# Turning the values and the attention weights by transposing DMAs instead of TensorE, in a two-layer hybrid block

## The chip, the core and the metric

The kernel runs on one core of a Trainium2 chip. A core has five engines that work side by side, each on its own list of instructions in a fixed order: TensorE (PE in the profile: matrix products, its weight loads are the row PEld), VectorE (DVE), ScalarE (ACT), GpSimd (POOL) and SyncE (SP), which here only issues DMAs. Engines wait for each other by semaphores. SBUF is the working memory with 128 partitions; PSUM takes what TensorE writes. The metric is the time of one execution on the device in microseconds; lower is better.

## The reference

The computation is a block of two layers on 272 tokens (16 learned ones and 256 of the input) with 1024 features, all in float32. In each layer the normalized input goes through one wide projection, and its parts feed three branches:

```
rq, rk, rv, rg, hq, hf, hi, hg, dq, dk, dv, mg = split(rms_norm(h) @ w_in)
o_ret = retention(rq, rk, rv, rg)        # 4 heads, values rv
o_hg  = hgrn2(hq, hf, hi, hg)            # 8 heads, a gated recurrence, values hi
o_da  = diff_attention(dq, dk, dv)       # 8 heads: w = softmax(s0) - lam * softmax(s1), then w @ dv
y = sum over the branches of sigmoid(mg_n) * (o_n @ w_branch_n)
h = h + y @ w_out
h = h + conv_ffn(rms_norm(h))            # 5632 wide in, causal convolution of 3, silu gate, 2816 wide out
```

Behind the second layer comes a last normalization. Each branch multiplies some matrix of weights over tokens with its values (`rv`, `hi`, `dv`), so the values are needed with tokens on partitions. The projections come out with features on partitions.

## The kernel before

**The main stream.** All large products run through `products`. A product's weights come as 128x128 tiles, in the order that `ORDER` and `_turns` write out; eight tiles are one chunk of 512 KB. `_Weights.next` (lines 623 to 647) loads a chunk into one of three "wraw" buffers by a DMA on SyncE's queue, ScalarE rounds it to "whi" and VectorE makes the rest, "wlo" (four buffers of each). Three matrix products per tile (lines 912 to 914: high by high, high by low, low by high) keep float32 accuracy. A pair of output tiles takes 16 weight tiles and lands in one of two "main" buffers in PSUM.

**The order.** No instruction is issued as the code meets it. `_Plan.add` notes each operation with its engine, a price and a due time (`key`), and finds what it depends on from the tiles and places it touches (`_span`). `order` (lines 451 to 559) then runs a list schedule: each engine takes what can start first, and of these what is due first, as long as a buffer of each tag is free. Small products on TensorE are due 3 us later than their key, or 8 us earlier when they can stand beside another small one. The prices are in `_Engine` (lines 580 to 604); a copy on GpSimd is taken as 0.04 + 2.45e-3 n us for n elements a partition, a DMA as 0.06 us and its bytes at 360 GB/s, and its result as there 2.0 us after that; a hand-off between engines costs 0.4. The order that comes out is fixed in the program. On the chip an engine whose next instruction isn't ready waits.

**The small work.** It is put in behind projections by the marks in `ORDER` ("+ret" begins the retention heads, "!ret" says where they must end). `behind` chains the pieces of a group: in "da" and "ret" a piece starts only when the last but one is done, so two heads are in flight. `settle` spreads their due times.

**What the change touches.**
- `values` (line 1378): a pair of value tiles (two times 128 features, 272 tokens) is copied out of PSUM into "vsrc", of which there are two buffers. `to_tokens` (line 948) then transposes the first 256 tokens in four blocks on TensorE into a PSUM bank "vt", and ScalarE copies it in two pieces into "vt" or "rvt". The last 16 tokens go another way (`tails`, `tail_tokens`). There are 12 such sets a layer: four each of `rv`, `hi` and `dv`.
- `da_head` (line 1263): the scores (line 1280, tile "ds"), the two softmaxes, whose difference is left in "two_a" on queries by keys (line 1300), `turn` (lines 1304 to 1308), which transposes three 128x128 blocks on TensorE into a bank "wt", two copies on ScalarE into the tile "wts", then the products with the values into "do", the norm of the head (`sub_norm`, with a sum over partitions on GpSimd) and the result in "da". Eight heads a layer, in two groups of four.
- `split_blocks` at the mark "*b2": the two halves of "da" become "b2hi" and "b2lo", which the products of the third branch ("b2") read: for the first eight tiles of a pair the first half, then the second.
- `ret_tail` and `ret_head` (lines 1000 and 1015): the products of the last 16 tokens, copied to `st["ro"]`, and those of the heads, both through the two "acc" banks.
- `SLOTS` (line 39): 14 large buffers shared by most tiles of the mixer and the feed-forward half, among them "vt", "dq", "da", "b2hi", "ghi".

Of the kernel before, what the change touches and what calls it, by code (L numbers as in the profile page):

```python
# [12 lines left out]
F32 = mybir.dt.float32  # L13
F32R = mybir.dt.float32r
U8 = mybir.dt.uint8
AF = mybir.ActivationFunctionType
ALU = mybir.AluOpType
PSUM = bass.MemoryType.PSUM
# [2 lines left out]
P = 128  # L21
DEPTH = 2
META = 16
SEQ = 256
T = META + SEQ
# [10 lines left out]
TAIL = T - 2 * P  # L36
BANK = 512
CHUNK_TILES = 8
SLOTS = 14
LEAD = 6.0  # L40
MARGIN = 12.0
EARLY = 12.0
# [313 lines left out]
class _Plan:  # L356
# [26 lines left out]
    def _span(self, ap):  # L383
        step = ap.ap[0][0]
        lo = ap.offset % step
        hi = lo + 1 + sum((n - 1) * abs(s) for s, n in ap.ap[1:])
        if ap.tensor.name in self.psum:

            lo, hi = lo // BANK * BANK, -(-hi // BANK) * BANK
        return ap.tensor.name, lo, hi  # L390

    def add(self, engine, run, cost, outs, ins, func=None):
# [271 lines left out]
def _trace(ctx, tc, plan, a, depth, probe):  # L664
    nc = tc.nc
# [18 lines left out]
    def new(pool_, shape, dt, tag, bufs, name):  # L684
        serial[0] += 1
        return plan.tile(pool_, shape, dt, tag, bufs, f"{name}_{serial[0]}")
# [16 lines left out]
    def temp2(tag, bufs=2):  # L703
        return temp(2 * T, tag, bufs).rearrange("p (a t) -> p a t", a=2)

    def bank(name):
        return new(bp, [P, 512], F32, "bank", 2, name)
# [34 lines left out]
    ident = const[:, C_IDENT : C_IDENT + P]  # L742
# [201 lines left out]
    def split(hi, lo, x):  # L944
        act.activation(hi, x, AF.Copy)
        tt(lo, x, hi.bitcast(F32), SUB)

    def to_tokens(src, vt, e):

        pt = bank("vt").rearrange("p (f c e) -> p f c e", f=2, c=2)  # L950
        for f in range(2):
            for c in range(2):
                pe.transpose(pt[:, f, c, :], src[:, f, c * P : (c + 1) * P], ident)
        for f in range(2):
            act.activation(vt[:, :, e + f * P : e + (f + 1) * P], pt[:, f], AF.Copy)

    def tail_tokens(tails):

# [21 lines left out]
    for li in range(depth):  # L980
# [19 lines left out]
        def ret_tail():  # L1000

            q, k = (st[n][:, :, 2 * P :].unsqueeze(1).to_broadcast([P, 2, 4, TAIL]) for n in ("rq", "rk"))
            ks = temp(P, "tw")
            twice = lambda t: t.rearrange("p (e h t) -> p e h t", e=2, h=4)
            pool.tensor_copy(twice(ks), k)
            s1 = bank("s1")[:, :P]
            pe.matmul(twice(s1), ks, q, start=True, stop=True)
            w = temp(P, "tw")
            tt(w, s1, const[:, C_DECT : C_DECT + P], MUL)
            o = acc_bank("ro")[:, :P]  # L1010
            pe.matmul(o, st["rvs"], w, start=True, stop=True)
            st["ro"] = temp(P, "tw")
            act.activation(st["ro"], o, AF.Copy)

        def ret_head(hd):
            q, k, vt, gate = st["rq"], st["rk"], st["rvt"], st["rg"]
            if hd == 0:
                st["dec"] = slot4("dec")
                sync.dma_start(st["dec"].rearrange("p h t -> p (h t)"), a["dec"])
            dec = st["dec"][:, hd, :]  # L1020

            s1 = bank("s1")
            a1 = temp(T + P + TAIL, "wts")
            parts = ((0, t0, t0, dec[:, t0:]), (P, P, T, dec[:, : P + TAIL]))
            for k0, q0, at, _ in parts:
                pe.matmul(s1[:, at : at + T - q0], k[:, hd, k0 : k0 + P], q[:, hd, q0:], start=True, stop=True)
                plan.hold(a1)
            for _, q0, at, by in parts:
                tt(a1[:, at : at + T - q0], s1[:, at : at + T - q0], by, MUL)
            os = [acc_bank("ro") for _ in range(2)]  # L1030
            sq = temp2("sum", 1)
            for e in range(2):
                o = os[e]
                ec = slice((hd * 2 + e) % 4 * P, (hd * 2 + e) % 4 * P + P)
                v = vt[(hd * 2 + e) // 4]
                pe.matmul(o[:, t0:T], v[:, 0, ec], a1[:, t0:T], start=True, stop=False)
                pe.matmul(o[:, P:T], v[:, 1, ec], a1[:, T : T + P + TAIL], start=False, stop=True)
            for e in range(2):
                i = (e * 4 + hd) * TAIL
                tt(os[e][:, 2 * P : T], os[e][:, 2 * P : T], st["ro"][:, i : i + TAIL], ADD)  # L1040
            for e in range(2):
                act.activation(sq[:, e, t0:], os[e][:, t0:T], AF.Square)
            tt(sq[:, 0, t0:], sq[:, 0, t0:], sq[:, 1, t0:], ADD)
            r = temp(T, "hr")
            inverse(r[:, t0:], sq[:, 0, t0:], 2 * P)
            for e in range(2):
                g = gate[:, hd * 2 + e, t0:]
                y = temp(T, "ho")[:, t0:]
                tt(y, os[e][:, t0:T], r[:, t0:], MUL)
                tt(g, y, g, MUL)  # L1050
# [212 lines left out]
        def da_head(b, hd):  # L1263
            q, k, vt, out = st[f"dq{b}"], st[f"dk{b}"], st[f"dvt{b}"], st[f"da{b}"]
            scale = DA_DH ** -0.5

            a1 = temp(T + P + TAIL, "wts")
            pool.tensor_copy(a1[:, :META], st[f"dw{b}"][:, hd * META : (hd + 1) * META])
            tiles = ((META + P, T, 0), (META, META + P, T))
            sb = [temp(2 * T, tag) for tag in ("two_a", "two_b")]  # L1270
            ss = [bank("ds") for _ in range(2)]
            red = temp(12, "dm")
            nm, sm, cf = (red[:, 4 * i : 4 * i + 4].rearrange("p (t m) -> p t m", m=2) for i in range(3))


            def scores():
                for q0, nk, at in tiles:
                    for m in range(2):
                        half = slice(64 * m, 64 * m + 64)
                        nc.tensor.matmul(ss[m][:, at : at + nk], q[half, hd, q0 : q0 + P], k[half, hd, :nk], start=True, stop=True)  # L1280

            plan.add("pe", scores, 0.95, [x[:, : T + P + META] for x in ss], [q[:, hd, :], k[:, hd, :]])
            plan.hold(*sb, a1)
            for i, (q0, nk, at) in enumerate(tiles):
                mask = const[:, C_MASK + T - nk : C_MASK + T]
                for m in range(2):
                    cols = slice(at, at + nk)
                    dve.tensor_tensor_reduce(out=sb[m][:, cols], in0=ss[m][:, cols], in1=mask, scale=1.0,
                                             scalar=-3e38, op0=ADD, op1=ALU.max, accum_out=nm[:, i, m : m + 1])
            ts(nm, nm, -scale, None, MUL)  # L1290
            for i, (q0, nk, at) in enumerate(tiles):
                for m in range(2):
                    p = sb[m][:, at : at + nk]
                    act.activation(p, p, AF.Exp, bias=nm[:, i, m : m + 1], scale=scale, accum_out=sm[:, i, m : m + 1])
            dve.reciprocal(cf, sm)
            tt(cf[:, :, 1], cf[:, :, 1], nlam[:, li : li + 1].to_broadcast([P, 2]), MUL)
            for i, (q0, nk, at) in enumerate(tiles):
                p0, p1 = (x[:, at : at + nk] for x in sb)
                ts(p1, p1, cf[:, i, 1:2], None, MUL)
                stt(p0, p0, cf[:, i, 0:1], p1, MUL, ADD)  # L1300
            w = sb[0]
            wt = bank("wt")

            def turn(wt=wt, w=w):
                for i, c in enumerate((0, P, T)):
                    nc.tensor.transpose(wt[:, i * P : (i + 1) * P], w[:, c : c + P], ident)

            plan.add("pe", turn, 0.33, [wt[:, : 3 * P]], [w[:, : T + P]])
            act.activation(a1[:, META + P : T + P], wt[:, : 2 * P], AF.Copy)
            act.activation(a1[:, META : META + P], wt[:, 2 * P : 3 * P], AF.Copy)  # L1310

            for g, c in ((0, 2 * P), (1, T + P)):
                pool.tensor_copy(st[f"dt{b}"][:, g, hd, :], w[:, c : c + TAIL])
            o = acc_bank("do")
            ec = slice(hd * P, hd * P + P)
            pe.matmul(o[:, t0:T], vt[:, 0, ec], a1[:, t0:T], start=True, stop=False)
            pe.matmul(o[:, P + META : T], vt[:, 1, ec], a1[:, T : T + P], start=False, stop=True)
            for g, c in ((0, 2 * P), (1, P)):
                act.activation(st[f"do{b}"][:, g, hd, :], o[:, c : c + TAIL], AF.Copy)
            sub_norm(out[:, hd, t0 : 2 * P], o[:, t0 : 2 * P])  # L1320
# [56 lines left out]

        def values(ps, vt, e):

            src = temp2("vsrc")  # L1380
            evacuate(src, ps)
            plan.key += 2.0
            to_tokens(src, vt, e)
            return src
# [234 lines left out]
```

## Time and profile before

| | |
|---|---|
| time, median of 3 runs | 1308.54 us (1308.46 to 1308.67) |
| the profiled execution | 1308.31 us, of which the span from first to last instruction is 1306.5 us |
| granted TensorE clock | 0.999 |
| value sets, attention heads | 24 and 16 in all |
| share of the span in which the DMA engines moved data | 49% |

A row of a group or a tile tells the line, the engine, the operation, what it writes and reads, the count and the durations in nanoseconds (a mean, or least, median and most). A row of the waits tells who waited for whom, for how many microseconds in total, how many times, and the longest. A row of the timeline gives the start and the length in microseconds; with "x4" several equal ones are merged. All that goes through the helper stands under line 604, so the tiles' names tell what it is. TensorE's matmuls overlap, so their spacing counts and not their length.

### The profile page before, as it was taken

The numbers are of one execution on the slowest core, as the hardware profiler recorded it, in microseconds if no ns is written. First come the engines' busy times: TensorE is split into PE (matmuls) and PEld (weight loads), VectorE is DVE, ScalarE is ACT, GpSimd is POOL, SyncE is SP. The second block draws the span as 40 slices with busy tenths as digits, with TensorE's granted clock in tenths as the row PEclk, the third lists the DMA queues.
The fourth block names the chain that finished last, engine by engine and source line by source line (L and its number), as shares of the span: only waits on it lengthen the run. The fifth ranks groups of instructions, "written<-read, shape, count | busy, mean of one in ns | idle before, by whom it ended". The sixth has DMA issues, their size and how long they took to land.

```text
span 1306.5 us, 28679 instructions
## 1 busy us (share of the span) xinstructions
PE 1294.6 (99%) x11774; PEld 1265.6 (97%) x11774; DVE 958.4 (73%) x1589; ACT 800.5 (61%) x1328; POOL 168.6 (13%) x204
## 2 busy tenths in 40 slices
PE   9999999999999999999999999999999999999998
PEld 9999999999999999999999999999999999999986
DVE  7675777698586789886575767876985867898843
ACT  6846454756576567666456564657565765776643
POOL 5001111222122020000030011012130220200000
PEclk9999999999999999999999999999999999999999
DMA  7644543443534545555555445444445445465553
GB/s 271 200 148 161 169 156 130 162 146 123 184 136 158 181 156 178 189 167 185 175 177 188 164 148 177 148 147 160 146 144 180 139 162 202 145 208 196 200 189 111
DMA packets 60755, 219.06 MB, mean 168 GB/s; under 512 B 6864, under 2 KB 6992, under 8 KB 60624
## 3 DMA queue, kind: packets, MB, share of 16 engines
q1 hardware_dynamic: 60336, 216.71, 49.0%
q8 instruction: 92, 1.51, 0.5%
q10 hardware_dynamic: 288, 0.52, 0.1%
q14 instruction: 39, 0.32, 0.1%
HBM read 216.16 MB, written 1.05 MB: 166 GB/s over the span
## 4 chain that ended last, share of the span: by engine, by line
PE 92%; DVE 5%; issue 1%; ACT 1%; DMA 0%; SPq 0%; DVEq 0%; ACTq 0%
PE main L912 27%; PE main L914 27%; PE main L913 26%; PE fo L1420 2%; PE fo L1419 2%; PE fo L1418 2%; DVE two_b L604 1%; PE lev L1096 1%; DVE two_a L604 1%; DVE wlo L604 1%; PE ds L1280 1%; PE vt L604 1%; PE ro L604 1%; PE ho L604 1%; PE do L604 1%
## 5 line engine op out<-in xcount | busy, mean ns | idle before, releaser
L912 PE MATMUL main<-xh,whi 128*128 128x272 f32 (+1 forms) x2368 | 682.0, 288 | 0.0
L913 PE MATMUL main<-xl,whi 128*128 128x272 f32 (+1 forms) x2368 | 672.5, 284 | 1.5 <-DVE xl L604 1.5
L914 PE MATMUL main<-xh,wlo 128*128 128x272 f32 (+1 forms) x2368 | 673.1, 284 | 0.9 <-DVE wlo L604 0.5
L604 DVE TENSOR_TENSOR wlo<-wraw,whi 128x1024 fp32r<-128x1024 f32 (+1 forms) x411 | 501.9, 1227 | 202.9 <-ACT whi L604 202.2
L604 ACT ACTIVATE whi<-wraw 128x1024 fp32r<-128x1024 f32 (+1 forms) x411 | 427.6, 1043 | 244.5 <-PE main L913 167.1
L914 PEld LDWEIGHTS main<-xh,wlo 128*128 128x128 f32 x2368 | 445.8, 188 | 2.7 <-DVE wlo L604 2.7
L913 PEld LDWEIGHTS main<-xl,whi 128*128 128x128 f32 x2368 | 446.1, 188 | 2.2 <-DVE xl L604 1.9
L912 PEld LDWEIGHTS main<-xh,whi 128*128 128x128 f32 x2368 | 446.1, 188 | 1.0
L604 DVE SCALAR_TENSOR_TENSOR two_b<-main,small,two_b 128x256 f32<-128x256 f32 (+2 forms) x144 | 65.3, 486 | 24.8 <-ACT two_b L604 23.1
L604 POOL PARTITION_ALL_REDUCE hr<-hsq x36 | 67.5, 1886 | 117.0 <-ACT hsq L604 116.2
L604 POOL TENSOR_TENSOR y<-h,rstd 128x272 f32<-128x272 f32 x32 | 34.6, 1112 | 318.1 <-ACT rstd L604 318.1
L604 ACT ACTIVATE two_b<-main,small 128x272 f32<-128x272 f32 (+1 forms) x72 | 37.3, 566 | 24.3 <-PE main L914 23.3
L912 PE MATMUL main<-ghi,whi 128*128 128x272 f32 x176 | 51.0, 290 | 0.0
L913 PE MATMUL main<-glo,whi 128*128 128x272 f32 x176 | 50.6, 287 | 0.0
L914 PE MATMUL main<-ghi,wlo 128*128 128x272 f32 x176 | 50.3, 286 | 0.0
L604 POOL COPY tails<-vsrc 128x32 f32<-128x32 f32 x32 | 10.1, 330 | 225.0 <-ACT vsrc L604 224.9
L912 PE MATMUL main<-b0hi,whi 128*128 128x272 f32 (+1 forms) x128 | 37.9, 296 | 0.0
L912 PE MATMUL main<-b1hi,whi 128*128 128x272 f32 (+1 forms) x128 | 37.8, 296 | 0.0
L912 PE MATMUL main<-yhi,whi 128*128 128x272 f32 (+1 forms) x128 | 36.4, 284 | 0.0
L914 PE MATMUL main<-yhi,wlo 128*128 128x272 f32 (+1 forms) x128 | 36.4, 284 | 0.0
L913 PE MATMUL main<-b1lo,whi 128*128 128x272 f32 (+1 forms) x128 | 36.3, 284 | 0.0
L914 PE MATMUL main<-b1hi,wlo 128*128 128x272 f32 (+1 forms) x128 | 36.3, 284 | 0.0
(236 smaller groups left out, 1915.9 us busy)
## 6 DMA issues: line engine op xcount, KB each, us to landing
wraw<-in_w SPq DMA_DIRECT2D x402, 512.0 KB, 3.3
h<-in_h SPq DMA_DIRECT2D x4, 272.0 KB, 5.3
dec<-in_dec SPq DMA_DIRECT2D x2, 544.0 KB, 4.2
wraw<-in_w SPq DMA_DIRECT2D x4, 256.0 KB, 4.5
const<-in_const SPq DMA_DIRECT2D x1, 937.0 KB, 6.1
gain<-in_gl SPq DMA_DIRECT2D x1, 512.0 KB, 5.5
out<-y ACTq DMA_DIRECT2D x2, 256.0 KB, 3.0
out<-y SPq DMA_DIRECT2D x2, 256.0 KB, 2.9
```

The costliest lines, as they stand in the source:

```text
L604: self.plan.add(self.name, lambda: f(*args, **kw), cost, outs, ins, args[2] if method == "activation" else None)
L912: nc.tensor.matmul(o, wh, hi, start=first, stop=False)
L913: nc.tensor.matmul(o, wh, lo, start=False, stop=False)
L914: nc.tensor.matmul(o, wl, hi, start=False, stop=last)
L1096: nc.tensor.matmul(o, keys, x, start=True, stop=True)
L1280: nc.tensor.matmul(ss[m][:, at : at + nk], q[half, hd, q0 : q0 + P], k[half, hd, :nk], start=True, stop=True)
L1418: nc.tensor.matmul(o, gh, wh, start=False, stop=False)
L1419: nc.tensor.matmul(o, gl, wh, start=False, stop=False)
L1420: nc.tensor.matmul(o, gh, wl, start=False, stop=end)
```

## The change

Both turns leave TensorE. A float32 tile is seen as pairs of 16-bit halves. Two copies on GpSimd (four in an attention head, whose source has two pieces) part it into a plane of the low halves and a plane of the high halves ("apart"). Two transposing DMAs on SyncE's queue, one for each plane, write the blocks transposed ("turned"). Two copies on GpSimd put the halves together again in the place where ScalarE had copied from PSUM. The PSUM banks "vt" and "wt" of these steps and the copies by ScalarE are gone.

With it: "apart" and "turned" are buffers of the tag "vsrc", which has now four instead of two; each large buffer is as big as two of them, and `SLOTS` goes from 14 to 13. `_span` halves the places of 16-bit tiles. A retention head's first product now waits until the copy of the tail's product is done.

```diff
-SLOTS = 14
+SLOTS = 13
@@ _span
+        if ap.dtype == U16:
+            lo, hi = lo / 2, hi / 2
@@
+    def planes(name, n):
+        return new(tp, [P, 4 * T], U16, "vsrc", 4, name)[:, : 2 * n].rearrange("p (i x) -> p i x", i=2)
+
+    def halves(t):
+        return t.bitcast(U16).rearrange("p (x two) -> p x two", two=2)
+
     def to_tokens(src, vt, e):
-        pt = bank("vt").rearrange("p (f c e) -> p f c e", f=2, c=2)
-        for f in range(2):
-            for c in range(2):
-                pe.transpose(pt[:, f, c, :], src[:, f, c * P : (c + 1) * P], ident)
-        for f in range(2):
-            act.activation(vt[:, :, e + f * P : e + (f + 1) * P], pt[:, f], AF.Copy)
+        apart, turned = planes("apart", 4 * P), planes("turned", 4 * P)
+        for i in range(2):
+            pool.tensor_copy(apart[:, i].rearrange("p (c f x) -> p c f x", c=2, f=2),
+                             halves(src.rearrange("p f t -> p (f t)"))[:, :, i].rearrange("p (f t) -> p f t", f=2)[:, :, : 2 * P].rearrange("p f (c x) -> p c f x", c=2))
+        for i in range(2):
+            sync.dma_start(turned[:, i].rearrange("p (b x) -> p b x", x=P), apart[:, i], transpose=True)
+        for i in range(2):
+            pool.tensor_copy(vt.bitcast(U16).rearrange("p c (x two) -> p c x two", two=2)[:, :, e : e + 2 * P, i], turned[:, i].rearrange("p (c x) -> p c x", c=2))
@@ ret_tail
             act.activation(st["ro"], o, AF.Copy)
+            st["rot"] = plan.ops[-1]
@@ ret_head
                 pe.matmul(o[:, t0:T], v[:, 0, ec], a1[:, t0:T], start=True, stop=False)
+                plan.queue(plan.ops[-1], st["rot"])
@@ da_head
             w = sb[0]
-            wt = bank("wt")
-            def turn(wt=wt, w=w):
-                for i, c in enumerate((0, P, T)):
-                    nc.tensor.transpose(wt[:, i * P : (i + 1) * P], w[:, c : c + P], ident)
-            plan.add("pe", turn, 0.33, [wt[:, : 3 * P]], [w[:, : T + P]])
-            act.activation(a1[:, META + P : T + P], wt[:, : 2 * P], AF.Copy)
-            act.activation(a1[:, META : META + P], wt[:, 2 * P : 3 * P], AF.Copy)
+            apart, turned = planes("apart", 3 * P), planes("turned", 3 * P)
+            for i in range(2):
+                for c, n, at in ((0, 2 * P, P), (T, P, 0)):
+                    pool.tensor_copy(apart[:, i, at : at + n], halves(w[:, c : c + n])[:, :, i])
+            for i in range(2):
+                sync.dma_start(turned[:, i].rearrange("p (b x) -> p b x", x=P), apart[:, i], transpose=True)
+            for i in range(2):
+                pool.tensor_copy(halves(a1[:, META : T + P])[:, :, i], turned[:, i])
@@ values
-            src = temp2("vsrc")
+            src = temp2("vsrc", 4)
```

1 line of the change is left out of this document (added).

## The prediction

> **What bounds the kernel now.** I read the page first (busy time, the chain that ended last), then the waits, and then the timeline of the places the change touches.
>
> ```profile
> span 1306.5 us, 28679 instructions
> PE 1294.6 (99%) x11774; PEld 1265.6 (97%) x11774; DVE 958.4 (73%) x1589; ACT 800.5 (61%) x1328; POOL 168.6 (13%) x204
> PE 92%; DVE 5%; issue 1%; ACT 1%; DMA 0%; SPq 0%; DVEq 0%; ACTq 0%
> ```
>
> TensorE is busy 99% of the span and carries 92% of the chain. A TensorE instruction that goes away is worth its time, and a microsecond in which TensorE waits is lost. GpSimd has room, 13% busy. What feeds TensorE is the weight stream:
>
> ```profile
> SPq L604 <- DVE wlo L604: 780.0, 279, 7.7
> ACT whi L604 <- PE main L913: 167.1, 141, 3.0
> ACT whi L604 <- DMA wraw<-in_w: 17.2, 14, 3.4
> PEld main L914 <- DVE wlo L604: 2.7, 9, 0.5
> ```
>
> ```profile
> q1 hardware_dynamic: 60336, 216.71, 49.0%
> ```
>
> The columns are total microseconds, times, longest. SyncE's queue mostly stands before a load whose raw buffer is still being split (780 us). ScalarE waits for TensorE to free a split buffer ten times as long as for a load, so the weights are ahead of their use, and TensorE hardly waits for them (2.7 us). The transfers of that queue fill the DMA engines to 49%.
>
> **What goes.** The sets of transposes, with the ordinary matmuls around them:
>
> ```profile
> L604 PE MATMUL vt<-const,vsrc x96: 270/272/329, 77.8 to 994.4; 128*128 128x128 f32 x96
> L1306 PE MATMUL wt<-const,two_a x48: 270/272/330, 294.0 to 1047.3; 128*128 128x128 f32 x48
> 160.14 0.29 PE L913 MATMUL main<-xl,whi 128*128 128x272 f32 x1
> 160.26 0.29 PE L914 MATMUL main<-xh,wlo 128*128 128x272 f32 x1
> 160.39 0.60 PE L604 MATMUL vt<-const,vsrc 128*128 128x128 f32 x4
> 160.74 0.37 PE L912 MATMUL main<-xh,whi 128*128 128x272 f32 x1
> 293.90 0.29 PE L914 MATMUL main<-b0hi,wlo 128*128 128x272 f32 x1
> 294.03 0.49 PE L1306 MATMUL wt<-const,two_a 128*128 128x128 f32 x3
> 294.27 0.37 PE L912 MATMUL main<-b0hi,whi 128*128 128x272 f32 x1
> PEld wt L1306 <- DVE two_a L604: 3.1, 6, 0.7
> ```
>
> Matmuls overlap, so the price is read from start to start. From 160.26 to 160.74 is 0.48 us where two ordinary matmuls are 0.12 apart: a values set costs 0.36 us. There are 96 / 4 = 24 sets: 8.6 us. An attention set costs 294.27 - 293.90 - 0.12 = 0.25 us, 48 / 3 = 16 sets: 4.0 us. The waits of these sets for the weights' last product (3.1 us, 6 times) go with them. Sum of the gain: 15.7 us. ScalarE loses the copies out of PSUM, but it is not the bound, and I count nothing for it.
>
> **What comes.** Each turn becomes copies on GpSimd (parting), two transposing DMAs on SyncE's queue, and copies on GpSimd (joining). The nearest rows:
>
> ```profile
> 178.82 0.21 POOL L604 COPY tails<-vsrc 128x32 f32<-128x32 f32 x1 [6.45 <-ACT vsrc L604]
> 824.25 0.29 POOL L604 COPY tw<-rk 128x128 f32<-128x128 f32 x1
> 170.59 1.05 POOL L604 COPY tails<-vsrc 128x32 f32<-128x32 f32 x1 [6.19 <-ACT vsrc L604]
> 170.28 1.28 DVE L604 TENSOR_TENSOR hq<-hq,he 128x1088 f32<-128x1088 f32 x1
> L604 POOL TENSOR_TENSOR y<-h,rstd 128x272 f32<-128x272 f32 x32 | 34.6, 1112 | 318.1 <-ACT rstd L604 318.1
> small<-in_small SPq DMA_DIRECT2D x1, 16.0 KB, 1.7
> wraw<-in_w SPq DMA_DIRECT2D x402, 512.0 KB, 3.3
> DMA to landing us min/median/max: 3.0/3.3/6.4
> L604 SPq DMA_DIRECT2D wraw<-in_w x406: 327/328/716, 1.6 to 1283.7; - x136
> L604 ACT ACTIVATE vsrc<-main x6: 624/627/628, 155.4 to 193.1; 128x544 f32<-128x544 f32 x6
> ```
>
> A GpSimd copy: 0.21 us at 32 elements and 0.29 at 128, so 0.18 + 0.83 ns an element. That gives 0.39 us at 256, 0.50 at 384 and 0.61 at 512. The copy at 170.59 took 1.05 us instead of 0.21: it started inside VectorE's product of two SBUF tiles and ended with it. VectorE is 73% busy; I take half of such a delay, 0.42 us, for each copy. The ends are no delay, and the two-input row (1112 ns at 272, so 4.1 ns an element, 2.1 us at 512).
>
> A transposing DMA is nowhere in the trace. A plane is 128 KB (values) or 96 KB. The fastest row is the 16 KB load, 1.7 us; the slowest on this queue is a weight load, 6.4 us. I take the ordinary weight load, 3.3 us: it moves more bytes, but the planes move in far smaller pieces. I take the two planes of a turn one after the other, 6.6 us, since both pass one queue. The ends are 1.7 + 0.33 (one issue) = 2.0 us and 2 x 6.4 = 12.8 us.
>
> [...]
>
> *Values.* Per layer 12 sets, 6 of them in one row, 155.4 to 193.1, 7.5 us apart. GpSimd gets 4 x (0.61 + 0.42) = 4.1 us a set, SyncE's queue 6.6 us: both fit in 7.5. The users come late enough:
>
> ```profile
> 81.50 0.21 POOL L604 COPY tails<-vsrc 128x32 f32<-128x32 f32 x1 [7.05 <-ACT vsrc L604]
> L604 PE MATMUL ho<-at,vt x64: 258/280/286, 106.1 to 920.7; 128*128 128x144 f32 x32, 128*128 128x128 f32 x16, 128*128 128x114 f32 x16
> L604 PE MATMUL ro<-wts,rvt x64: 284/332/395, 209.3 to 894.8; 128*128 128x144 f32 x32, 128*128 128x272 f32 x16, 128*128 128x258 f32 x16
> ```
>
> The second set of the gated recurrence is in SBUF by 81.5, and the first product with such values ("ho") starts at 106.1, 25 us later. The first retention product starts at 209.3 and reads the first two sets of its four, in SBUF at 170.6 and 178.8: 30 us. A turn of 4.1 + 6.6 us fits, and I count nothing. What hides it is this lead, and three of the four "vsrc" buffers a set; without it the next set stays in PSUM and TensorE stops. A weight load queued behind a transposing DMA that waits for GpSimd is late by the same time; the lead of the weights shown above hides single delays.
>
> *Attention heads.* Here the turn lies on a chain that is waited for:
>
> ```profile
> 292.93 0.37 DVE L604 SCALAR_TENSOR_TENSOR two_a<-two_a,dm,two_b 128x144 f32<-128x144 f32 x1
> 296.23 0.84 PE L604 MATMUL do<-wts,vt 128*128 128x272 f32 x4
> 366.31 0.85 PE L1280 MATMUL ds<-dk,dq 64*128 64x272 f32 x6
> 411.38 1.29 DVE L604 TENSOR_TENSOR b2lo<-da,b2hi 128x1088 fp32r<-128x1088 f32 x1
> 420.27 0.29 PE L912 MATMUL main<-b2hi,whi 128*128 128x272 f32 x1
> 1061.30 1.23 DVE L604 TENSOR_TENSOR b2lo<-da,b2hi 128x1032 fp32r<-128x1032 f32 x1
> 1067.38 0.28 PE L912 MATMUL main<-b2hi,whi 128*128 128x258 f32 x1
> ```
>
> Before, from the weights' end (293.30) to the head's output product (296.23) is 2.9 us. After: the first plane's two copies 0.39 + 0.29 + 2 x 0.42 = 1.5 (the second plane's lie beside the first transfer); SyncE standing before a load, half of 780 / 279 us = 1.4; transfers 6.6; joining the second plane 0.50 + 0.42 = 0.9; hand-offs 0.3. Together 10.7 us, so a head grows by 7.8 us (ends: 0.7 + 2.0 + 0.5 + 0.3 - 2.9 = +0.6, and +15 with 12.8 for the transfers and full delays).
>
> At most two heads are in flight, so a group of four takes two rounds and grows by 15.6 us. The second group's result is ready at 412.7. The third branch's products begin at 420.3 and reach that half after 8 tiles x 3 x 0.12 = 3 us, at 423.2: 10.5 us of cover, less 1.5 that TensorE no longer spends on turns meanwhile, 9.0. In the second layer it is ready at 1062.5 and needed at 1070.2: 7.7 - 1.5 = 6.2 us. TensorE so stops for 15.6 - 9.0 = 6.6 and 15.6 - 6.2 = 9.4 us, 16 together.
>
> The first group has no such end, but TensorE's order is fixed beforehand by the planner's prices (lines 585 to 603, and 2.0 us after a DMA). With them this chain is 2 x 1.02 (parting) + 0.6 + 2.0 (the second DMA) + 0.98 (joining) + 4 x 0.4 (hand-offs) = 7.2 us, 3.5 short of mine, so TensorE meets the output product too early. Before, its prices were short by about 1 us a head (1.9 of 2.9), and 16 turns cost the 3.1 us above: 0.2 of the difference. Once per pair at full price would be 4 x 3.5 = 14 us, a fifth per head 8 x 3.5 x 0.2 = 5.6; I take the middle, 10 us. On GpSimd a joining copy that waits for its DMA holds up what stands behind it, the tail copies and the other head's all-reduce; that is in the upper end, not in the sum.
>
> *The rest.* The edit that lets a retention head wait for the copy of the tail's output holds back two products by at most the copy, 0.5 us once a layer; the planner has ordinary matmuls to put there: 0, up to 1. Thirteen slots: the feed-forward half holds six "ghi" and six "glo", 12, and I count no more elsewhere: 0; were the cover gone, a result would stay in PSUM.
>
> **Sum**: 1308.3 (the profiled execution, 0.2 below the median 1308.5) - 15.7 + 16 + 10 = 1318.6, say 1319 us.
>
> **The rivals.** *The turn is as quick as a small load* (other side). With 2.0 us for the pair, the head's chain is 1.5 + 1.4 + 2.0 + 0.9 + 0.3 = 6.1, +3.2. Two rounds, 6.4 us, stay within the cover in layer one and miss it by 0.2 in layer two, and the planner's 7.2 us is enough: 1308.3 - 15.7 = 1292.6, say 1294. For it: the queue's DMA engines are half idle, and only the transfer has to be quick. Against it: even a plain 512 KB load takes 3.3 us. The point where it decides: the loss is 4g - 15.2 (the two covers) + 2.9(g - 4.3) for a head grown by g (2.9 being 10 / 3.5, and 4.3 the planner's 7.2 - 2.9), and it equals 15.7 at g = 6.3, a pair of 5.1 us. [...]
>
> *Both cancel*: g near 6.3, 1306 to 1311.
>
> *SyncE's queue becomes the bound.* At 6.4 us a plane a values set holds the queue 12.8 us where 7.5 are there; six sets miss 32 us. The weight loads stand behind them; three raw buffers at 1306 / 406 = 3.2 us a load cover 10, so 22 us a layer are lost. The heads grow by 14.0, which by the formula above loses 41 + 28 against the gain of 15.7: 1308 + 44 + 53 = some 1405 us. For it: one queue in order. Against: a plain load's issue holds SyncE 0.33 us only.
>
> *GpSimd is late*: at 2.1 us a copy a set needs 8.4 us for parting where 7.5 are there, and a head grows by some 3 more (4.1 ns an element, full delays): by the formula about 1340.
>
> **Chances.** Forecast (1311 to 1345) 0.40, quick turn 0.27, cancelling 0.08, queue 0.20, GpSimd 0.05. Range 1293 to 1380: it takes in the quick turn and leaves out most of the queue's case; the forecast's own is 1311 to 1345. A change under 0.2% (2.6 us) can't be told from none. Faster 0.27, same 0.08, slower 0.65.
>
> **What would show it.** Right: no "vt" and no attention "wt" transposes on TensorE, 15 us less busy; TensorE waits at "do" and before "b2hi"; a head's weights-to-output time near 11 us; GpSimd's copies 0.4 to 1.0 us. Wrong: transposing DMAs landing under 2.5 us (faster), or holding SyncE for microseconds, with "wraw" waited for by ScalarE (much slower); a wait at "main" for a PSUM buffer during the values would contradict my zero there.

## The result and the profile after

The changed kernel takes 1326.68 us (median of 5 runs, 1323.02 to 1328.93), the kernel before 1308.54 us (1308.46 to 1309.06): a ratio of 1.013, with a 95% interval of 1.0118 to 1.0141. It is 18.1 us slower. The execution that was profiled took 1323.02 us, the fastest of the five, 14.7 us more than the profiled execution before (1308.31). What is read below from the two traces accounts for the 14.7 us; the rest of the 18.1 is in executions that have no trace.

First the page of the changed kernel, the lines that answer to those shown of before.

```profile
span 1321.2 us, 28630 instructions
...
PE 1284.1 (97%) x11630; PEld 1253.8 (95%) x11630; DVE 985.0 (75%) x1589; ACT 778.7 (59%) x1250; POOL 334.8 (25%) x396
...
PE 81%; DVE 7%; POOL 4%; ACT 3%; DMA 3%; issue 1%; SPq 0%; DVEq 0%; ACTq 0%; POOLq 0%
```

TensorE lost 144 matmuls and is 10.5 us less busy, and yet its share of the chain that ended last fell from 92% to 81%. GpSimd (4%) and the DMA (3%) now stand on that chain. VectorE, which got no instruction more, is 26.6 us busier.

Next the waits of TensorE in the changed kernel (total microseconds, times, longest). The prediction showed, on its weight loads, only 2.7 us for a weight half and 3.1 us for the turns.

```profile
PE main L915 <- ACT b2hi L607: 10.7, 2, 6.0
PE do L607 <- DVE tw L607: 4.7, 2, 3.2
PE lev L1109 <- DVE hf L607: 3.1, 2, 1.6
PE vm L607 <- POOL tails L607: 2.5, 4, 1.1
PE main L916 <- DVE b2lo L607: 1.7, 2, 1.1
PE do L607 <- POOL wts L607: 1.7, 3, 0.7
PE lev L1109 <- DVE hq L607: 1.0, 1, 1.0
```

Two groups stand out. The third branch's products wait for the second group of heads, once in each layer: 10.7 + 1.7 = 12.4 us. And products in the section of the values wait for VectorE and for GpSimd's tail copies (those of the recurrence, "lev", and the transposes of the last 16 tokens' values, "vm"): 3.1 + 1.0 + 2.5 = 6.6 us, with shorter ones of the kind ("ho" 0.8 among them) 8.2 us. The prediction's sum had the first and not the second. Before, the waits of this engine over 0.5 us in all were these three, beside one at the start:

```profile
PE wt L1306 <- DVE two_a L604: 1.6, 4, 0.5
PE main L913 <- DVE xl L604: 1.5, 2, 1.1
...
PE do L604 <- DVE tw L604: 0.8, 1, 0.8
```

The transposing DMAs (tile "turned"; durations of the issue, then the time to landing), and after them one of GpSimd's groups of copies, kept apart by shape:

```profile
L607 SPq DMA_TRANSPOSE turned<-apart x80: 1183/1196/2983, 74.8 to 1068.0; - x80
...
DMA to landing us min/median/max: 2.3/3.7/6.5
```

```profile
L607 POOL COPY apart<-vsrc 128x512 uint16<-128x512 uint16 x48 | 45.0, 957 | 144.9 <-ACT vsrc L607 144.7
```

A transposing DMA holds SyncE for 1.2 us, where a weight load held it for 0.33, and lands 3.7 us after its issue. None lands in less than 2.3 us, and in the median a plane takes about as long as a weight load with at least four times its bytes (3.6 us in this trace). The planes move in small packets: SyncE's queue moves 39424 packets and 9.44 MB more than before (99760 and 226.15 MB), 239 bytes a packet, where before a packet had 3.6 KB in the mean. In the run below with the heads alone attention planes land in 3.5 us in the median and 2.3 at least; the 20 values planes that the changed kernel issues before 290 us land in 3.9 and 2.4.

The first head, in the timeline of the changed kernel (start, length):

```profile
292.98 0.40 POOL L607 COPY apart<-two_a 128x256 uint16<-128x256 uint16 x1 [5.76 <-DVE two_a L607]
...
293.60 1.94 POOL L607 COPY apart<-two_a 128x128 uint16<-128x128 uint16 x3 [0.22 <-DVE two_a L607]
...
293.93 1.20 SPq L607 DMA_TRANSPOSE turned<-apart  x1
...
295.80 1.19 SPq L607 DMA_TRANSPOSE turned<-apart  x1
...
296.29 0.63 POOL L607 COPY wts<-turned 128x384 uint16<-128x384 uint16 x1 [0.47 <-DMA turned<-apart]
...
298.35 2.44 DVE L607 TENSOR_TENSOR wlo<-wraw,whi 128x1024 fp32r<-128x1024 f32 x2
298.49 2.57 POOL L607 COPY apart<-two_a 128x128 uint16<-128x128 uint16 x2 [0.22 <-DVE two_a L607]
...
301.01 0.63 POOL L607 COPY wts<-turned 128x384 uint16<-128x384 uint16 x1
...
302.46 0.84 PE L607 MATMUL do<-wts,vt 128*128 128x272 f32 x4
```

The first plane is joined 2.4 us after its DMA was issued. The second plane's joining copy starts at 301.01, 5.2 us after its own (295.80), and it did not wait for the transfer to the end: GpSimd came to it straight from the parting copies of the next head, which took 2.57 us for two (298.49) beside VectorE's products "wlo" of two SBUF tiles (298.35 to 300.79). The output product follows at 302.46. Over all 16 heads the way from the weights' end to that product is 10.57 us in the mean; before it was 2.75. This head is not the typical one. Over the 15 heads whose planes can be told apart from those of the values, the two transfers take 6.3 us in the mean, from the first issue to the second landing, since the second plane's DMA is issued 2.5 us after the first's; from the last landing to the copy that joins it 0.9 us go by.

What the wait before the third branch does, in layer 1. First the timeline of TensorE (its last row is of layer 2), then the windows (length, busy time and count of TensorE and of its weight loads, of VectorE, ScalarE, GpSimd; granted clock; DMA share; GB/s).

```profile
428.54 0.59 PE L915 MATMUL main<-b2hi,whi 128*128 128x272 f32 x1 [4.66 <-ACT b2hi L607]
430.19 0.60 PE L916 MATMUL main<-b2lo,whi 128*128 128x272 f32 x1 [1.06 <-DVE b2lo L607]
430.59 0.43 PE L917 MATMUL main<-b2hi,wlo 128*128 128x272 f32 x1
430.81 0.43 PE L915 MATMUL main<-b2hi,whi 128*128 128x272 f32 x1
...
434.67 0.30 PE L917 MATMUL main<-b2hi,wlo 128*128 128x272 f32 x1
...
1079.27 0.49 PE L607 MATMUL do<-tw,vs 128*128 128x128 f32 x2 [3.18 <-DVE tw L607]
```

```profile
423.60:427.80 4.20, 0.29 (x3) 0.07 (x1) 1.57 (x3) 4.16 (x6) 0.41 (x2) 1.00 0.00 0
427.85:434.65 6.80, 5.05 (x20) 4.75 (x21) 2.29 (x2) 0.64 (x1) 0.00 (x0) 0.50 0.46 157
434.70:440.00 5.30, 5.30 (x44) 5.30 (x44) 4.56 (x7) 2.78 (x3) 0.00 (x0) 1.00 0.16 39
1079.80:1090.00 10.20, 3.56 (x15) 3.27 (x16) 3.46 (x5) 2.88 (x6) 2.32 (x4) 0.50 0.31 103
```

TensorE stands for 4.66 us, and the granted clock falls to 0.50, 4.0 us into the stop. When work comes again, matmuls follow each other every 0.227 us (430.59 to 430.81, to 434.67) instead of every 0.12, until 434.67: the clock is back at 1.00, 6.1 us after work began. Layer 2 has the same, for over 10 us; there the wait of a tail's product (3.18 us, at 1079.27) leads straight into that for the second group (6.0 us). From 430.59 to 434.67 are 18 matmuls at 0.107 us too much, 1.9 us; the same reading of 1087.40 to 1089.98 in layer 2 gives 1.2 us.

So the profiled difference adds up: -12.6 (40 sets of transposes, at the prediction's prices) - 2.4 (waits of before that are gone or shorter, "wt" and "xl") + 12.4 (before the third branch) + 5.6 ("do", 4.7 + 1.7 against 0.8) + 8.2 (the values' section) + 3.1 (half clock) = 14.3 us, against 14.7 measured.

### The profile page after: what moved, and what is told of

Same layout as the page of the kernel before. It is cut to its first block, busy times and chain, and to the rows that moved or that the text cites. A ratio compares the mean times of both kernels' runs of the same rounds, so it can differ in the third digit from the quotient of the medians.

```text
span 1321.2 us, 28630 instructions
## 1 busy us (share of the span) xinstructions
PE 1284.1 (97%) x11630; PEld 1253.8 (95%) x11630; DVE 985.0 (75%) x1589; ACT 778.7 (59%) x1250; POOL 334.8 (25%) x396
## 3 DMA queue, kind: packets, MB, share of 16 engines
q1 hardware_dynamic: 99760, 226.15, 56.7%
## 4 chain that ended last, share of the span: by engine, by line
PE 81%; DVE 7%; POOL 4%; ACT 3%; DMA 3%; issue 1%; SPq 0%; DVEq 0%; ACTq 0%; POOLq 0%
PE main L915 24%; PE main L916 24%; PE main L917 24%; DVE wlo L607 2%; POOL apart L607 2%; DMA turned<-apart 2%; PE fo L1430 2%; PE fo L1431 2%; PE fo L1432 2%; PE ds L1293 1%; PE ho L607 1%; PE lev L1109 1%; PE ro L607 1%; ACT whi L607 1%; DVE two_b L607 1%
## 5 line engine op out<-in xcount | busy, mean ns | idle before, releaser
L607 DVE TENSOR_TENSOR wlo<-wraw,whi 128x1024 fp32r<-128x1024 f32 (+1 forms) x411 | 514.9, 1258 | 183.0 <-ACT whi L607 180.4
L607 POOL PARTITION_ALL_REDUCE hr<-hsq x36 | 70.2, 1966 | 81.4 <-ACT hsq L607 81.4
L607 POOL COPY apart<-vsrc 128x512 uint16<-128x512 uint16 x48 | 45.0, 957 | 144.9 <-ACT vsrc L607 144.7
L607 POOL COPY apart<-two_a 128x256 uint16<-128x256 uint16 x64 | 40.6, 660 | 58.6 <-DVE two_a L607 58.6
L915 PE MATMUL main<-b2hi,whi 128*128 128x272 f32 (+1 forms) x128 | 38.4, 300 | 10.7 <-ACT b2hi L607 10.7
L607 POOL COPY vt<-turned 128x512 uint16<-128x512 uint16 x32 | 33.4, 1056 | 26.5 <-DMA turned<-apart 26.2
L916 PE MATMUL main<-b2lo,whi 128*128 128x272 f32 (+1 forms) x128 | 38.3, 299 | 1.7 <-DVE b2lo L607 1.7
L917 PE MATMUL main<-b2hi,wlo 128*128 128x272 f32 (+1 forms) x128 | 37.7, 295 | 0.0
```

The source lines that it names most:

```text
L607: self.plan.add(self.name, lambda: f(*args, **kw), cost, outs, ins, args[2] if method == "activation" else None)
L915: nc.tensor.matmul(o, wh, hi, start=first, stop=False)
L916: nc.tensor.matmul(o, wh, lo, start=False, stop=False)
L917: nc.tensor.matmul(o, wl, hi, start=False, stop=last)
```

## The experiments

Each is compared with the kernel before on the same chip; its median lay between 1308.46 and 1308.62 in all of them. My theory was that the heads' longer chain makes the loss and the values' part is a gain; the rivals stand in each expectation.

**Values alone, and heads alone.** The old transposes were put back in `da_head`, and in the other run in `to_tokens`:

```diff
# values_only: da_head as before
-            apart, turned = planes("apart", 3 * P), planes("turned", 3 * P)
...
+            wt = bank("wt")
+            plan.add("pe", turn, 0.33, [wt[:, : 3 * P]], [w[:, : T + P]])
...
# attention_only: to_tokens as before
-        apart, turned = planes("apart", 4 * P), planes("turned", 4 * P)
...
+        pt = bank("vt").rearrange("p (f c e) -> p f c e", f=2, c=2)
...
```

> Values turned by DMA as in the changed kernel, attention weights turned on TensorE as before. Theory (the loss is the attention heads' longer chain, which ends in TensorE's wait before the third branch's products; the values' turn lies beside other work): 24 sets x 0.36 us less on TensorE and no wait before the third branch, 1298 to 1303 us. Rival (the values' copies and transposing DMAs cost as well, by late weight loads or late consumers): 1308 us or more.

> Attention weights turned by DMA as in the changed kernel, values on TensorE as before. Theory (heads' chain): both waits before the third branch's products stay, and the 8.6 us of the values' sets are back on TensorE: 1328 to 1337 us. Rival (values and attention share the loss): under 1322 us.

Measured: values alone 1305.82 us (1303.55 to 1306.51; ratio 0.9977, 0.9967 to 0.9987), heads alone 1321.72 us (1320.96 to 1322.30; 1.0099, 1.0082 to 1.0116). The heads carry the loss, and their trace has the waits before "b2" (12.4 us) and the half clock of the changed kernel. But both numbers are off: the values bring 2.8 us of the 8.6 that their transposes cost, the heads alone lose 13.1 where I expected some 20 or more, and the two together (10.3) explain 18.1 badly. The trace of the values alone shows where their gain is eaten. First its timeline, then one VectorE product from it and the same one from the kernel before (busy time, mean ns):

```profile
169.74 0.76 PE L1109 MATMUL lev<-hq,hf 128*32 128x32 f32 x64 [0.90 <-DVE hq L607]
...
180.21 0.73 PE L1109 MATMUL lev<-hq,hf 128*32 128x16 f32 x64 [1.49 <-DVE hf L607]
...
740.37 1.88 POOL L607 COPY vt<-turned 128x512 uint16<-128x512 uint16 x1 [0.16 <-DMA turned<-apart]
...
741.53 1.24 DVE L607 TENSOR_TENSOR hq<-hq,tot 128x544 f32<-128x544 f32 x1
```

```profile
L607 DVE TENSOR_TENSOR hq<-hq,tot 128x544 f32<-128x544 f32 x12 | 10.4, 865 | 0.0
```

```profile
L604 DVE TENSOR_TENSOR hq<-hq,tot 128x544 f32<-128x544 f32 x12 | 8.6, 717 | 0.0
```

The same product of two SBUF tiles lasts 865 ns in the mean instead of 717, and the first matmuls of a level of the recurrence wait for it and for its like ("hf"). The mean hides two cases. The eight of the twelve that no GpSimd copy meets last 712 to 722 ns, as before; the four that start while one of GpSimd's copies runs last 1034 to 1242 ns, and each ends 0.5 to 0.6 us after that copy (741.53 above: the copy ends at 742.25, the product at 742.77). So in these four VectorE stands until the copy is through. The prediction had counted that VectorE delays GpSimd, and not that GpSimd delays VectorE.

**The values' copies on ScalarE.** The DMAs stay, and the four copies of a values set leave GpSimd; the heads are as before.

```diff
# to_tokens, against values_only
-            pool.tensor_copy(apart[:, i].rearrange(...), halves(...)...)
+            act.activation(apart[:, i].rearrange(...), halves(...)..., AF.Copy)
...
-            pool.tensor_copy(vt.bitcast(U16).rearrange(...)[...], turned[:, i].rearrange(...))
+            act.activation(vt.bitcast(U16).rearrange(...)[...], turned[:, i].rearrange(...), AF.Copy)
```

> Values turned by DMA, attention weights on TensorE, and the four copies of a values set moved from GpSimd to ScalarE. Theory (GpSimd's copies hold up VectorE's products of two SBUF tiles, which the gated recurrence's small products on TensorE wait for): VectorE's hq by tot product falls back from 0.87 to 0.72 us, TensorE's waits before lev go, 1299 to 1304 us. Rival (those waits come from the transposing DMAs or from an out-of-date order): the waits stay, 1304 to 1308 us; more if ScalarE's roundings of the weights get late.

Measured: 1301.03 us (1297.95 to 1302.81; ratio 0.9938, 0.9925 to 0.9950). The product by line and shape, from this kernel:

```profile
L607 DVE TENSOR_TENSOR hq<-hq,tot 128x544 f32<-128x544 f32 x12 | 8.6, 718 | 0.0
```

It is back at 718 ns, the same transposing DMAs notwithstanding, and the gain is 7.6 us of 8.6. So for the values the copies on GpSimd are the cause, not the transfers. This version, with the heads on TensorE as before, is 25.7 us faster than the changed kernel.

**No transposing DMA in the heads.** GpSimd's copies stay, and the joining copies read the parted planes. The attention weights are left unturned here.

```diff
# against attention_only
-            for i in range(2):
-                sync.dma_start(turned[:, i]..., apart[:, i], transpose=True)
...
-                pool.tensor_copy(halves(a1[:, META : T + P])[:, :, i], turned[:, i])
+                pool.tensor_copy(halves(a1[:, META : T + P])[:, :, i], apart[:, i])
```

> Attention weights parted and joined by GpSimd as in the run with attention alone, but the joining copies read the parted planes and no transposing DMA is issued: the weights are left unturned, so the attention's output is another. Theory (the DMA pair with its queue is some 6 of the 7.8 us by which a head grew): from weights to output product 4 to 6 us, no wait before the third branch's products, 1304 to 1310 us. Rival (the copies and VectorE's hold-ups make the head late): still above 1314 us.

Measured: 1303.91 us (1301.78 to 1304.47; ratio 0.9961, 0.9947 to 0.9974), just under what I expected. The way from the weights to the output product is 5.30 us (9.93 with the DMAs), and TensorE waits for nothing before the third branch. Of the waits at the heads these are left:

```profile
PE do L607 <- POOL wts L607: 1.8, 1, 1.8
PE do L607 <- DVE tw L607: 1.5, 1, 1.5
```

The two transfers alone, 4.6 us a head, turn a gain of 4.7 us into a loss of 13.1. GpSimd's copies in the heads cost little by themselves.

**Idle time filled.** With the heads alone turned, constant products keep TensorE at work where it stood: 12 behind the tails' transpose and 20 before the awaited tile of the third branch.

```diff
# against attention_only
+    def filler(n, behind):
+        t = bank("fill")
+        def run():
+            for _ in range(n):
+                nc.tensor.matmul(t[:, :P], ones_d, ones_d, start=True, stop=True)
+        op = plan.add("pe", run, 0.214 * n, [t[:, :P]], [ones_d])
...
+                filler(12, [plan.ops[-1]])
...
+                fill = filler(20, [plan.main[-1], st["dax"]])
```

> The run with attention alone, with products of constants in TensorE's list where it waits for the last heads (12 behind the transpose of the tails, 20 before the waited-for tile). Theory (the half clock behind the wait comes from TensorE standing idle for some 4 us): the granted clock stays full and the third branch begins no later, 4 to 6 us less, 1315 to 1318 us. Rival (it comes from the transposing DMAs or the load): the half clock stays, 1321 us or more.

Measured: 1317.17 us (1316.43 to 1318.48; ratio 1.0066, 1.0052 to 1.0080), 4.6 us less than without the filling. Its timeline at the same place, and its windows:

```profile
423.67 4.63 PE L936 MATMUL fill<-ones_d 128*128 128x128 f32 x40
428.06 0.38 PE L915 MATMUL main<-b2hi,whi 128*128 128x272 f32 x1
...
430.77 0.29 PE L915 MATMUL main<-b2hi,whi 128*128 128x272 f32 x1
430.93 0.40 PE L916 MATMUL main<-b2lo,whi 128*128 128x272 f32 x1
```

```profile
423.60:435.00 11.40, 11.40 (x96) 11.31 (x96) 4.87 (x6) 7.91 (x8) 0.41 (x2) 1.00 0.35 119
1070.00:1090.00 20.00, 20.00 (x176) 20.00 (x175) 11.11 (x15) 13.06 (x18) 3.23 (x4) 1.00 0.31 109
```

The transposing DMAs are the same, and the clock stays at 1.00: the half clock comes from TensorE standing idle. The products at 428.06 are not the awaited ones yet. In both runs 48 products of the third branch need only the first half; in layer 1 the planner put 21 of them behind the filling. The 49th, the first that was waited for, starts at 430.77 in layer 1 (427.64 unfilled) and at 1081.96 in layer 2 (1083.83). So the filling moves more than the clock, and the 4.6 us are not the half clock's price alone. The spacing gives that price: unfilled, the 105 products from 429.29 on take 15.60 us and the 143 from 1085.10 on 19.17, where at the spacing of the kernel before they would take 12.9 and 16.7. The two stops cost some 5 us beside their own 12.4.

**The planner's prices.** Is the order bad because the planner doesn't know the long chain?

```diff
+            if outs[0].dtype == U16 or ins and ins[0].dtype == U16:
+                cost = 1.2 if method == "dma_start" else 0.18 + 0.83e-3 * n + 0.4
...
-            done = t + cost + (2.0 if e == "sp" else 0.0)
+            done = t + cost + (2.0 if e == "sp" else 0.0) + (0.5 if op.func == "turn" else 0.0)
```

> The changed kernel, with the planner told what the trace showed: a transposing DMA holds the queue 1.2 us and lands 2.5 us after, a copy of 16-bit halves takes 0.58 + 0.83e-3 n us. Theory: the small waits of TensorE at out-of-date places (some 10 us in all) shrink, the wait before the third branch stays: 1315 to 1323 us. Rival (the wrong prices cause the wait before the third branch too): under 1312 us.

Measured: 1331.58 us (1330.71 to 1332.87; ratio 1.0176, 1.0161 to 1.0192). A miss: it got slower. Its waits:

```profile
PE main L917 <- ACT b2hi L609: 12.7, 2, 6.5
PE do L609 <- POOL wts L609: 8.6, 3, 3.3
PE main L917 <- ACT vsrc L609: 3.1, 1, 3.1
```

With the true prices the chain from weights to output product got longer (13.49 us in the mean instead of 10.57) and the output products wait more, not less; a product of the main stream now also waits for a values tile to leave PSUM (3.1 us). That TensorE meets the output products too early because of outdated prices is not borne out. The edit changes the order of all engines, though, so it does not test TensorE's places by themselves.

**Earlier places for the second group.** `settle` spreads the jobs of a section; a job's due times start behind its own beginning by as many steps as jobs stand ahead of it, those counted that began long before.

```diff
                 begin = max(begin, mine[0][1])
+                i -= sum(x[1] < begin for x in mine)
```

> The changed kernel, but the due times of the second group of four heads begin at their own start and not six steps later, some 10 to 15 us earlier. Theory (heads' chain too long for the room before the third branch): the wait before the third branch goes in the first layer and shrinks in the second, and the half clock behind it with it: 1302 to 1314 us, with the head's time from weights to output product still near 10.5 us. Rival (waits elsewhere carry the loss): above 1320 us.

Measured: 1313.98 us (1312.89 to 1315.20; ratio 1.0041, 1.0026 to 1.0056), 12.7 us less than the changed kernel by the medians (7.8 by the two profiles), at the upper edge of what I expected. Layer 1 has no wait before the third branch any more; layer 2 still has one of 5.7 us. The chain itself is as long as in the changed kernel (10.62 us), so what it costs is a matter of when it starts.

**Buffers alone.**

```diff
# against the kernel before
-SLOTS = 14
+SLOTS = 13
...
+            st["rot"] = plan.ops[-1]
...
+                plan.queue(plan.ops[-1], st["rot"])
...
-            src = temp2("vsrc")
+            src = temp2("vsrc", 4)
```

> The kernel before with 13 large buffers, four vsrc buffers and the retention heads' wait for the tail's copy, and nothing turned by DMA. Theory (buffers and that wait cost nothing): 1308 to 1309.5 us. Rival (a missing large buffer moves work): 1310 us or more.

Measured: 1308.12 us (1307.67 to 1308.98; ratio 0.9998, 0.9988 to 1.0007). They cost nothing.

**The whole change with both cures.** The values' copies on ScalarE, alone and with the earlier places; the edits are those of the runs above, against the changed kernel.

```diff
# all_scalar, and all_scalar_early
-            pool.tensor_copy(apart[:, i].rearrange(...), ...)
+            act.activation(apart[:, i].rearrange(...), ..., AF.Copy)
...
# all_scalar_early only
+                i -= sum(x[1] < begin for x in mine)
```

> The whole change, with the values' four copies a set on ScalarE instead of GpSimd; the heads keep theirs on GpSimd. Theory (the heads' late result sets the time of both layers' attention sections, and the values' copies on GpSimd lengthen VectorE's products beside them and the heads' chains with them): the values then add nothing of their own, and the time is that of the attention part alone or a little under, 1316 to 1322; the products hq<-hq,tot at 544 elements last about 0.72 us. Rival (the 5 us that the values add on top of the attention part come from the shared SyncE queue, where the values' transposing DMAs stand): it stays at 1324 to 1328.

> As the run beside it, and the second group of heads in each layer gets its places in TensorE's order from its own beginning. Theory: both losses shrink, so the time lies under that of the earlier places alone (1314.0) by what the values' copies on GpSimd cost, 2 to 6 us: 1307 to 1312, no gain left over the kernel before, because layer 2 keeps its wait before the third branch (about 3 us or more, and half clock behind it). Rival (with GpSimd free the heads get quick enough): no wait of over 1 us before b2hi in either layer, 1298 to 1304.

Measured: 1312.83 us (1312.27 to 1318.00; ratio 1.0044, 1.0028 to 1.0060) and 1300.19 us (1296.86 to 1302.23; ratio 0.9934, 0.9914 to 0.9953). Both are under what the theory said. The first falls 8.9 us below the heads alone, nearly the 8.6 of the values' transposes: with the copies off GpSimd the two parts add up (-7.6 and +13.1 make +5.5, and +4.4 was measured), and my idea that a wait at the end of the section swallows whatever the values win falls. In the changed kernel the same 96 copies cost 13.9 us by the medians, 7.7 by the two profiles. In the second the rival held: no product waits for "b2hi" in either layer. From its page:

```profile
PE 1280.9 (99%) x11630; PEld 1252.5 (96%) x11630; DVE 963.9 (74%) x1589; ACT 831.1 (64%) x1344; POOL 228.9 (18%) x300
```

TensorE is busy 99% of the span again, 13.7 us less than before the change, and VectorE is back from 985 to 964 us. This version does all that the change set out to do and is 8.3 us faster than the kernel before.

**Controls for the order.** The earlier places in the kernel before, and with the values' part alone.

```diff
# before_early: before.  values_scalar_early: values_scalar
                 begin = max(begin, mine[0][1])
+                i -= sum(x[1] < begin for x in mine)
```

> The kernel before with one thing changed: the second group of heads gets its places in TensorE's order from its own beginning. It tells whether the order alone is worth anything, or only mends what the longer heads lost. Theory (before, the second group's result was 7 to 10 us early, so no wait is there to be mended): the same, 1306 to 1311. Rival (the crowded places cost the kernel before too): under 1305.

> The values turned by transposing DMAs with copies on ScalarE, the heads' weights turned on TensorE as before, and the earlier places for the second group of heads. Beside the run of the whole change with both edits (1300.2) it tells what the attention part is worth once nothing waits for its result. Theory (16 sets off TensorE at 0.25 us are 4.0 us): it is slower than that run by 2 to 5 us, 1301 to 1305. Rival (the attention part brings nothing even then, the order is what helps): it is at 1297 to 1300.

Measured: 1309.30 us (1309.02 to 1309.59; ratio 1.0005, 0.9996 to 1.0015) and 1301.88 us (1300.73 to 1303.13; ratio 0.9949, 0.9934 to 0.9964). The order is worth nothing by itself; it mends only what the longer heads lost. The heads' part on top of the values' (1301.88 to 1300.19) brings 1.7 us of its 4.0, within the spread of both. So the fastest two versions, the values alone with copies on ScalarE (1301.03) and the whole with both cures (1300.19), can't be told apart.

## Why the prediction was right, and where it was not

The forecast was slower, 1319 us; it is slower, 1326.7. Its main mechanism was there and some of its terms were well sized, but two steps failed. That the sum is only 8 us low is in part luck: the 10 us for the order are some 2.4 on the trace, and the values' 8.2 us and the half clock's 3.1 stood at nothing.

- *The gain, 15.7 us.* Right. The transposes are gone. That TensorE is only 10.5 us less busy, and not 15, fits the longer matmuls at half clock (0.43 us in layer 1 instead of 0.29); where the stops are mended it is 13.7 us less.
- *A head grows from 2.9 to 10.7 us.* Right: 10.57. The pair of transfers was put at 6.6 us and takes 6.3 in the mean, though not for the reason given. The second plane does not stand behind the first's transfer: its DMA is issued 2.5 us after the first's, once its copies are done and SyncE is free. SyncE's queue costs 1.2 us a head (1.4 foreseen), at the second plane and not at the first; this is the mean of the 16 heads with the values on TensorE. What the sum left out is GpSimd's queue: 0.9 us in the mean between the last landing and its joining copy, and up to 3.3, as the joining stands behind the next head's parting. I had put that into the upper end alone. That the transfers are what tips it is shown: without them a head needs 5.30 us, and the time is below the kernel before.
- *16 us before the third branch.* Right as a place, in both layers: 12.4 us, and with the tail's wait that leads into it in layer 2 (3.2 us) 15.6. That it comes so near is luck as well. In layer 1 the second half is ready 17.5 us later than before (430.1 instead of 412.7) and not 15.6, while TensorE has more to do until then: the planner put the first half of the next pair ahead, 48 products instead of the 24 counted, 3 us more of cover in each layer.
- *10 us for outdated places in TensorE's order.* This step failed. The waits at the output products grew by 5.6 us, most of it (4.7) at the tails' products "do<-tw"; without the 3.2 us that belong to the stop in layer 2 it is 2.4. And true prices made the kernel slower, not faster. What in the order does cost is another thing: the second group of heads starts late. Moved forward it gives back 12.7 us.
- *Values: "a turn fits, and I count nothing".* This step failed, and it is the largest miss. The lead of the values did hide the turns. The copies on GpSimd cost VectorE, whose products of two SBUF tiles stand until a running copy ends (717 ns alone, 1034 to 1242 behind a copy) with the recurrence waiting for them, and they hold up the tail copies in GpSimd's queue (TensorE's "vm" waits 2.5 us for those, and did not before). Taking them off GpSimd gives 13.9 us by the medians, 7.7 by the two profiles.
- *A stop costs its own length.* Nothing in the sum stood for the half clock behind it: 3.1 us in the profiled execution by the spacing of its matmuls, some 5 us in the run with the heads alone.
- *Buffers, slots, the retention wait: 0.* Right, 1308.12.
- *The rivals.* The quick turn fell: 6.3 us the pair instead of 2.0. SyncE's queue did not become the bound: the weights come a little later (ScalarE waits 36.6 us for loads instead of 17.2), but TensorE waits for a weight half for 1.2 us in all. The row of the changed kernel's waits:

```profile
ACT whi L607 <- DMA wraw<-in_w: 36.6, 20, 3.6
```

  GpSimd was late, not by its own 2.1 us a copy as that rival had it, but by what it does to its neighbour.

The prediction's formula put the break-even at a head of 2.9 + 6.3 = 9.2 us. The heads at 5.30 us gained and those at 9.93 lost, but with the second group's places moved a head of 9.77 us costs no wait before the third branch: the break-even belongs to one order, not to the kernel.

## What to carry to other kernels

Work taken off a full engine is worth its time only if what replaces it neither lengthens a chain that is waited for nor disturbs an engine that is on one: here the same transposing DMAs lost 18 us or won 8, depending on which engine made the copies beside them and on when the consumers were placed. Before copies go to an idle GpSimd, look which of VectorE's two-tile products run beside them and who waits for those: here such a product took 1034 to 1242 ns behind a copy and 717 without. And when a chain grows, look first at when it starts, before correcting a planner's prices: the start gave 12.7 us here, the prices cost 5.

## What the runs showed of the hardware

In the changed kernel a transposing DMA from SBUF to SBUF of 96 or 128 KB holds its queue's engine for 1.2 us in the median (1.18 to 2.98) and lands 2.3 to 6.5 us after issue, 3.7 in the median.

With the values alone turned, VectorE's product of two SBUF tiles of 128x544 that starts while GpSimd copies 16-bit halves ends 0.5 to 0.6 us after that copy and lasts 1034 to 1242 ns, where it lasts 712 to 722 with no copy beside it.

In the version with both cures the clock was halved behind a stop much shorter than those above: TensorE worked 1.41 of the 3.15 us before the clock fell, and its one idle stretch in them was 1.75 us. The windows, then the row that ends the stop:

```profile
342.00:345.15 3.15, 1.41 (x12) 1.22 (x11) 1.70 (x4) 2.80 (x7) 0.41 (x2) 1.00 0.67 245
345.20:348.50 3.30, 3.30 (x17) 3.30 (x16) 1.97 (x8) 2.78 (x6) 0.00 (x0) 0.50 0.20 79
```

```profile
344.64 0.41 PE L607 MATMUL ds<-dk,wts 128*128 128x64 f32 x2 [1.75 <-ACT wts L607]
```

In the heads without DMAs a similar stop of 1.54 us, with TensorE busy 2.46 of 4.00 us around it, left the clock at 1.00. What decides between the two is not settled.

One more thing stays open. With the values' copies on ScalarE, TensorE once stands in the midst of 64 like products of the recurrence, and the trace names nothing that it waits for ("issue"); this is in the version with all the change and the copies on ScalarE:

```profile
PE lev L1109 <- issue: 3.6, 1, 3.6
```

It is 3.6 us there, and behind it matmuls follow each other every 0.227 us (848.37 to 849.96); the values alone on ScalarE and the version with both cures have such a stop too (1.6 and 2.6 us), and behind the first of these the granted clock is 0.50 from 839.30 to 842.60. No run was made to find its cause.
